# Splitting five mixer results in place, and sharing the first norm's scaling between two engines

## The chip, the core and the metric

The kernel runs on one core of one Trainium2 chip. The metric is the device time of one execution in microseconds. Lower is better.

## The reference

The reference computes two transformer-like blocks in float32 over a sequence of 1024 tokens with a width of 1024. The change lies in the first block. Sixteen learned tokens are put in front of the sequence, one input projection makes all the raw inputs, three mixers work side by side on parts of it, and their results are concatenated, projected and normalized:

```python
q_a, f_a, i_a, g_a, z_b, xbc_b, dt_b, u_c = jnp.split(h @ w_in[l], split_idx, axis=-1)
y_a = hgrn2_mixer(q_a, f_a, i_a, g_a, ...)      # 384 columns
y_b = mamba2_mixer(z_b, xbc_b, dt_b, ...)       # 384 columns, ends in an RMS norm per group
y_c = s5_mixer(u_c, ...)                        # 256 columns, ends in y * sigmoid(y @ glu_w + glu_b)
mixed = jnp.concatenate([y_a, y_b, y_c], axis=-1) @ w_out[l]
h = layer_norm(ALPHA * h + mixed, ln1_g[l], ln1_b[l])
ff = jnp.square(jax.nn.relu(h @ w_mlp_in[l])) @ w_mlp_out[l]
h = layer_norm(ALPHA * h + ff, ln2_g[l], ln2_b[l])
```

The second block (a gated delta rule, a spatial gating branch and a gated feed-forward part) follows with the same kinds of operations. It is not touched.

## The kernel before

The tokens are worked in two halves, h = 0 (with the 16 learned tokens, 528 columns) and h = 1 (512 columns). Results of mixers lie with channels on the 128 partitions and tokens along the free dimension. The concatenated 1024 channels of one half are eight tiles of 128x512: tiles 0 to 2 from HGRN2, 3 to 5 from Mamba2, 6 and 7 from S5's gate (`glu`).

The large products are done in three passes over two-part numbers. A float32 operand is split into `hi`, a rounded copy made by ScalarE (`act`), and `lo`, the difference, made by VectorE (`tt`). `split` (L216) does this for activations, in a tile of the pool `xt` with 16 buffers; `weights` (L223) does it for each weight tile after its load (raw `wr` with 2 buffers, `wh` and `wl` with 3 each); `mm3` (L233) issues the three matrix products for one pair. In the profile, `ps<-wh,xt` and `ps<-wl,xt` are such products of the output projection, where the activations are the stationary operand; `ps<-xt,wh` and `ps<-xt,wl` are those of the input projections and the first MLP matrix. `px` tiles are banks for the small products of mixers, transposes and sums.

Before the change every mixer writes its result tile to a buffer in device memory, `Y1[h][j]`, with a DMA issued on POOL's queue (L686 for Mamba2, L950 for the gate, L512 for HGRN2). `load_y` (L1185) reads all eight back on SP's queue into `ev` tiles, of which there are 5, and splits each:

```python
for j in range(8):
    raw = self.ev()[:, :512]
    self.nc.sync.dma_start(raw, Y[j])
    xs.append(self.split(raw, 512, f))
```

`out_proj` (L1199) multiplies the eight operands by the output matrix in two column halves of four weight pairs; pair kp uses operands 2kp and 2kp + 1 for four groups of 128 tokens, 24 products for each pair. `ln_first` (L1272) is the first norm of half 0: row statistics on VectorE and POOL, a normalizing pass on ScalarE, transposes on TensorE, and then for each of eight channel tiles a scale and shift straight from the transposed bank: once on ScalarE into `x.hi` (rounded), once on VectorE into `r` (exact), and a VectorE subtraction into `x.lo`.

`run` (L1477) writes the program as coroutines that are interleaved by hand. The first input projection (`p1`) runs beside S5 and the mixers of half 0 (`seq(0)`), then come the gate of half 0 (`glu(0)`), `new_acc` and `load_y`, then the output projection beside the mixers of half 1 (`mix1(1)`), the first norm, and the MLP beside the rest of `mix1(1)`. This order gives priorities only. When the kernel is built, the framework orders the instructions of each engine by priority and by when their operands and buffers come free, so what the trace shows on a queue can stand in another order than the code. Each engine then runs its queue in that order.

Of the kernel before, what the change touches and what calls it, by code (L numbers as in the profile page):

```python
# [14 lines left out]
AF = mybir.ActivationFunctionType  # L15
ALU = mybir.AluOpType
# [61 lines left out]
class Op:  # L78


    def __init__(self, hi, lo):
        self.hi, self.lo = hi, lo
# [5 lines left out]
class Kb:  # L88
    NF = 24

    def __init__(self, tc, es, ap):
        self.tc, self.nc, self.ap = tc, tc.nc, ap
        self.es = es
        self.n = 0
        ec = es.enter_context
        self.cst = ec(tc.tile_pool(name="cst", bufs=1))
        self.xtp = ec(tc.tile_pool(name="xtp", bufs=16))
        self.wp = ec(tc.tile_pool(name="wp", bufs=4))
        self.accp = ec(tc.tile_pool(name="accp", bufs=8))
        self.mx = ec(tc.tile_pool(name="mx", bufs=1))  # L100
        self.sm = ec(tc.tile_pool(name="sm", bufs=2))
        self.ps = ec(tc.tile_pool(name="ps", bufs=4, space=PSUM))
        self.px = ec(tc.tile_pool(name="px", bufs=4, space=PSUM))
        self.dr = ec(tc.tile_pool(name="dr", bufs=1, space=DRAM))
        nc = self.nc
        self.Y1 = [self.dram([8, 128, 512], "Y1") for _ in range(2)]
        self.Y2 = [self.dram([8, 128, 512], "Y2") for _ in range(2)]
        k = self.cst.tile([128, 8], F32, tag="k", name="k")
        for i, v in enumerate((RMS_EPS, math.log(128.0 ** -0.5), 1.0, math.pi / 2, -0.5)):
            nc.vector.memset(k[:, i:i + 1], v)  # L110
        self.eps_rms, self.lnq, self.one, self.hpi, self.mhalf = (k[:, i:i + 1] for i in range(5))
# [455 lines left out]
    def mamba(self, h):  # L567
        nc = self.nc
        NT, R0 = HW[h], T0[h]
        xs = [self.t(528) for j in range(3)]  # L570
# [19 lines left out]
        b = self.bank()  # L590
# [4 lines left out]
        Y = [self.t(512) for j in range(3)]  # L595
        for c in range(c0, 5):
# [14 lines left out]
            if c > 0:  # L611
                for hd in range(6):
                    self.ts(W[hd // 3][:, hd % 3, :], W[hd // 3][:, hd % 3, :], ac[:, 6 * c + hd:6 * c + hd + 1], ALU.subtract, 0.0, ALU.min)
                b = self.bank()
# [10 lines left out]
            b = self.bank()  # L625
# [8 lines left out]
            b = self.bank()  # L634
# [6 lines left out]
            if c > 0:  # L641
                yb = self.bank()
                for hd in range(6):
                    j, o = hd // 2, 64 * (hd % 2)
# [29 lines left out]
        for j in range(3):  # L674
            b = self.bank()
            if j == 0:
                self.sums(b, [(ones, sq[0], al), (ones[lo], sq[1], lo)])
            elif j == 1:
                self.sums(b, [(left, sq[0], al), (self.blk, sq[1], al), (right, sq[2], al)])
            else:  # L680
                self.sums(b, [(ones[up], sq[1], up), (ones, sq[2], al)])
            r = self.t(512)
            self.act(r, b, AF.Ln, scale=1.0 / 192, bias=self.eps_rms)
            self.act(r, r, AF.Exp, scale=-0.5)
            self.stt(Y[j], Y[j], self.col(P_NW1 + j), r, ALU.mult, ALU.mult)
            nc.gpsimd.dma_start(self.Y1[h][3 + j], Y[j])  # L686
            yield


# [241 lines left out]
    def glu(self, h):  # L931
        nc = self.nc
        j0 = 2 if h == 0 else 66
        gw = self.t(512)
        nc.sync.dma_start(gw.rearrange("p (k c) -> p k c", k=2), self.ap["gluw"])
        y = [self.t(524)[:, :512] for j in range(2)]
        for j in range(2):
            nc.sync.dma_start(y[j].rearrange("p (t j) -> p t j", t=8), self.yT[j][:, :, j0:j0 + 64])
            self.act(y[j], y[j], AF.Gelu_apprx_tanh)
        for m in range(2):  # L940
            b = self.bank()
            for k in range(2):
                self.mm(b, gw[:, 256 * k + 128 * m:256 * k + 128 * m + 128], y[k], k == 0, k == 1)
            s = self.t(520)[:, :512]
            self.act(s, b, AF.Tanh, scale=0.5, bias=self.s5gb[:, m:m + 1])
            o = self.t(528)[:, :512]
            p = lambda x: x.rearrange("p (t j) -> p j t", t=8)
            self.stt(o.rearrange("p (j t) -> p j t", t=8), p(s), 1.0, p(y[m]), ALU.add, ALU.mult)
            self.ts(o, o, 0.5, ALU.mult)
            nc.gpsimd.dma_start(self.Y1[h][6 + m], o)  # L950
            yield


# [228 lines left out]
            yield  # L1182


    def load_y(self, Y, f=False):  # L1185
        xs = []
        for j in range(8):
            raw = self.ev()[:, :512]
            self.nc.sync.dma_start(raw, Y[j])
            xs.append(self.split(raw, 512, f))  # L1190
        return xs
# [80 lines left out]
    def ln_first(self, acc, gb, xs):  # L1272

        nc = self.nc
        for a in acc:
            mean, rs = self.stats([a[:, 0:512], a[:, 512:1024]], "ln")
            nm = self.s("nm", 1, 4)
            self.stt(nm, mean, -1.0, rs, ALU.mult, ALU.mult)
            self.act(a, a, AF.Identity, scale=rs, bias=nm)
        for k in range(8):  # L1280
            b = self.bank()
            for t in range(4):
                nc.tensor.transpose(b[:, 128 * t:128 * t + 128], acc[t][:, 128 * k:128 * k + 128], self.ident)
            g, s = self.col(P_LN + k), self.col(P_LN + 8 + k)
            r, x = self.ev()[:, :512], self.xt()
            self.act(x.hi[:, :512], b, AF.Identity, scale=g, bias=s)
            self.ts(r, b, g, ALU.mult, s, ALU.add)
            self.tt(x.lo[:, :512], r, x.hi[:, :512].bitcast(F32), ALU.subtract)
            xs.append(x)
        yield  # L1290
        for hf in range(2):
            c = slice(512 * hf, 512 * hf + 512)
            rows = [self.ev()[:, :512] for _ in range(2)]
            for i in range(2):
                nc.sync.dma_start(rows[i], gb[i:i + 1, c].to_broadcast([128, 512]))
            for t in range(4):
                a = acc[t][:, c]
                self.tt(a, a, rows[0], ALU.mult)
                self.tt(a, a, rows[1], ALU.add)
                yield  # L1300
# [176 lines left out]
    def run(self):  # L1477
# [7 lines left out]
        p1, m = self.p1(), self.s5s()  # L1485
# [4 lines left out]
        m = self.both(m, self.seq(0))  # L1490
# [4 lines left out]
        st(self.glu(0))  # L1495

        a0 = self.new_acc(half(ap["x"], 0))
        ys = self.load_y(self.Y1[0])
        m = self.mix1(1)
        st(self.out_proj(ys, ap["wo1"], a0), 99, m, 0.75, False)  # L1500
        x0 = []
# [8 lines left out]
        ys = self.load_y(self.Y1[1], True)  # L1510
        st(q)
        a1 = self.new_acc(half(ap["x"], 1))
        o, x0, x1 = self.out_proj(ys, ap["wo1"], a1), [], []
# [3 lines left out]
        p, m, n = self.p2(0, x0), self.mix2(0), self.ln(a1, l1, xs=x1)  # L1517
# [7 lines left out]
        ys, hs, x1, x0 = self.load_y(self.Y2[0], True), [], [], []  # L1525
        st(q)
        n = self.ln(a1, l2, out=self.X2[1], xs=x1)
        g = self.merge(0, ys, hs)
        st(g, 99, n, 1, False)
        a0 = self.new_acc(self.X2[0])  # L1530
        o = self.out_proj(hs, ap["wo2"], a0)
        st(o, 4, n, 1)
        st(o, 99, n, 2)
        p, m, n = self.p2(1, x1), self.mix2(1), self.ln(a0, l3, xs=x0)
# [6 lines left out]
        ys, hs, x1 = self.load_y(self.Y2[1], True), [], []  # L1541
# [8 lines left out]
        n, r = self.ln(a0, l4, out=half(ap["out"], 0)), self.ffn(1, x1, a1, ((0, 4), (4, 4), (8, 4), (12, 4), (16, 2), (18, 4)),  # L1550
                                                              self.ln_last(a1, l4, half(ap["out"], 1)))
# [165 lines left out]
```

## Time and profile before

| what | value |
|---|---|
| median of 3 runs | 2798.53 us |
| lowest and highest run | 2794.23 and 2805.1 us |
| the profiled execution: its time | 2800.17 us |
| the profiled execution: its span, first to last instruction | 2798.3 us |
| mean granted TensorE clock | 0.99 |
| instructions | 37325 |

The time of an execution is a little above its span, because it also holds what lies before the first and after the last instruction. Engines are named PE (TensorE's products), PEld (its weight loads), DVE (VectorE), ACT (ScalarE), POOL (GpSimd) and SP (SyncE, which issues most DMAs; SPq is its queue).

### The profile page before, as it was taken

The numbers are of one execution on the slowest core, as the hardware profiler recorded it, in microseconds if no ns is written. First come the engines' busy times: TensorE is split into PE (matmuls) and PEld (weight loads), VectorE is DVE, ScalarE is ACT, GpSimd is POOL, SyncE is SP. The second block draws the span as 40 slices with busy tenths as digits, with TensorE's granted clock in tenths as the row PEclk, the third lists the DMA queues.
The fourth block names the chain that finished last, engine by engine and source line by source line (L and its number), as shares of the span: only waits on it lengthen the run. The fifth ranks groups of instructions, "written<-read, shape, count | busy, mean of one in ns | idle before, by whom it ended". The sixth has DMA issues, their size and how long they took to land.

```text
span 2798.3 us, 37325 instructions
## 1 busy us (share of the span) xinstructions
PE 2722.5 (97%) x14176; PEld 2261.6 (81%) x14176; DVE 1793.5 (64%) x3321; ACT 1162.4 (42%) x1810; POOL 220.4 (8%) x365
## 2 busy tenths in 40 slices
PE   7999988999999999999999999999999999999997
PEld 7788776778878888877888878888788888888886
DVE  7668768777756654376645665534867657675566
ACT  4334444444442353263323333534545434444442
POOL 3121001000001112010100001100100000000000
PEclk9999999999999999999999999999999999999999
DMA  7432463323344543333333455434234533343332
GB/s 213 130 98 84 138 186 106 117 87 102 111 146 153 164 151 122 121 116 118 120 95 122 141 161 182 142 125 136 83 108 148 170 98 110 109 143 98 98 95 79
DMA packets 138036, 351.55 MB, mean 126 GB/s; under 512 B 26779, under 2 KB 40641, under 8 KB 137857
## 3 DMA queue, kind: packets, MB, share of 16 engines
q1 hardware_dynamic: 113712, 295.34, 34.4%
q0 software_dynamic: 16672, 48.50, 5.1%
q10 hardware_dynamic: 7473, 5.34, 0.7%
q8 instruction: 111, 1.82, 0.3%
q14 instruction: 68, 0.56, 0.1%
HBM read 296.84 MB, written 51.69 MB: 125 GB/s over the span
## 4 chain that ended last, share of the span: by engine, by line
PE 76%; issue 8%; DVE 8%; DMA 4%; ACT 3%; POOL 1%; SPq 0%; DVEq 0%; POOLq 0%; ACTq 0%
PE ps L204 68%; PE px L204 7%; DVE f L192 2%; ACT f L189 2%; DVE wl L192 1%; DVE ta L192 1%; DVE f L195 1%; DMA ev<-gt 1%; PE px L1268 1%; DMA f<-rows 1%; DVE acc L195 1%; DMA wr<-in_w 1%; DMA cx<-qkv 1%; ACT wh L189 1%; DMA f<-in_xT 0%
## 5 line engine op out<-in xcount | busy, mean ns | idle before, releaser
L204 PE MATMUL ps<-xt,wh 128*128 128x512 f32 (+1 forms) x3616 | 1098.3, 382 | 8.9 <-ACT wh L189 8.7
L192 DVE TENSOR_TENSOR wl<-wr,wh 128x1024 fp32r<-128x1024 f32 (+3 forms) x431 | 521.9, 1211 | 581.7 <-ACT wh L189 566.3
L204 PE MATMUL ps<-wh,xt 128*128 128x512 f32 (+3 forms) x2624 | 804.3, 380 | 8.2 <-ACT xt L189 4.9
L189 ACT ACTIVATE wh<-wr 128x1024 fp32r<-128x1024 f32 (+3 forms) x431 | 452.2, 1050 | 863.6 <-PE ps L204 772.7
L204 PEld LDWEIGHTS ps<-xt,wh 128*128 128x128 f32 x3616 | 665.3, 189 | 123.4 <-ACT wh L189 8.6
L204 PE MATMUL ps<-xt,wl 128*128 128x512 f32 (+1 forms) x1808 | 683.9, 378 | 6.6 <-DVE wl L192 6.6
L204 PEld LDWEIGHTS ps<-wh,xt 128*128 128x128 f32 (+1 forms) x2624 | 486.0, 188 | 95.1 <-ACT xt L189 8.1
L204 PE MATMUL ps<-wl,xt 128*128 128x512 f32 (+3 forms) x1312 | 496.8, 379 | 1.1 <-DVE wl L192 1.0
L204 PEld LDWEIGHTS ps<-xt,wl 128*128 128x128 f32 x1808 | 341.8, 189 | 69.2 <-DVE wl L192 8.6
L204 PE MATMUL ps<-f,wh 128*128 128x512 f32 x960 | 293.5, 386 | 0.0
L204 PEld LDWEIGHTS ps<-wl,xt 128*128 128x128 f32 (+1 forms) x1312 | 247.3, 189 | 43.7 <-DVE wl L192 3.3
L189 ACT ACTIVATE f<-f 128x512 f32<-128x512 f32 (+6 forms) x300 | 178.8, 614 | 206.2 <-DVE f L192 62.6
L204 PE MATMUL px<-f,f 128*128 128x128 f32 (+8 forms) x1832 | 203.3, 259 | 20.4 <-DVE f L192 12.4
L204 PEld LDWEIGHTS ps<-f,wh 128*128 128x128 f32 x960 | 179.9, 187 | 36.3
L189 ACT ACTIVATE ev<-ps 128x512 f32<-128x512 f32 (+4 forms) x303 | 169.3, 561 | 64.7 <-PE ps L204 58.2
L192 DVE TENSOR_TENSOR acc<-acc,ps 128x512 f32<-128x512 f32 x192 | 131.0, 684 | 89.4 <-PE ps L204 88.4
L204 PE MATMUL ps<-f,wl 128*128 128x512 f32 x480 | 184.8, 385 | 0.0
L204 PEld LDWEIGHTS px<-f,f 128*128 128x128 f32 (+2 forms) x1192 | 133.7, 180 | 57.4 <-issue 25.3
L192 DVE TENSOR_TENSOR f<-f,f 128x256 f32<-128x256 f32 (+5 forms) x244 | 129.0, 549 | 38.4 <-ACT f L189 36.5
L189 ACT ACTIVATE xt<-ev 128x512 fp32r<-128x512 f32 x131 | 82.4, 629 | 152.4 <-DVE ev L192 147.3
L195 DVE SCALAR_TENSOR_TENSOR ev<-ev,p,ev 128x512 f32<-128x512 f32 x176 | 132.3, 752 | 2.7 <-ACT ev L189 0.6
L192 DVE TENSOR_TENSOR xt<-ev,xt 128x512 fp32r<-128x512 f32 x124 | 86.1, 697 | 50.7 <-ACT xt L189 50.3
(223 smaller groups left out, 2047.9 us busy)
## 6 DMA issues: line engine op xcount, KB each, us to landing
wr<-in_w SPq DMA_DIRECT2D x93, 512.0 KB, 3.8
wr<-in_wup SPq DMA_DIRECT2D x88, 512.0 KB, 3.5
wr<-in_wmi SPq DMA_DIRECT2D x64, 512.0 KB, 3.6
wr<-in_wmo SPq DMA_DIRECT2D x64, 512.0 KB, 3.7
wr<-in_wdn SPq DMA_DIRECT2D x44, 512.0 KB, 3.4
wr<-in_wo SPq DMA_DIRECT2D x32, 512.0 KB, 3.8
Y<-f POOLq DMA_DIRECT2D x32, 256.0 KB, 2.6
ev<-Y SPq DMA_DIRECT2D x32, 256.0 KB, 3.7
```

The lines of the kernel that those rows point to most:

```text
L189: self.nc.scalar.activation(out=out, in_=in_, func=func, **kw)
L192: self.nc.vector.tensor_tensor(out=out, in0=a, in1=b, op=op)
L195: self.nc.vector.scalar_tensor_tensor(out=out, in0=a, scalar=s, in1=b, op0=op0, op1=op1)
L204: self.nc.tensor.matmul(out, lhsT, rhs, start=start, stop=stop)
L1268: nc.tensor.transpose(b[:, 128 * t:128 * t + 128], acc[t][:, 128 * k:128 * k + 128], self.ident)
```

## The change

Two things are changed. For half 0 Mamba2's three results and the gate's two are split where they are made and kept as operands in `xt` tiles; they are not written to device memory, and `load_y` takes them from a table, so that it loads and splits only tiles 0 to 2. Half 1 is left as it was. In `ln_first`, for every second channel tile, the exact scaled copy `r` is made by ScalarE and not by VectorE.

```diff
+        self.ysp = {}
...
             self.stt(Y[j], Y[j], self.col(P_NW1 + j), r, ALU.mult, ALU.mult)
-            nc.gpsimd.dma_start(self.Y1[h][3 + j], Y[j])
+            if h == 0:
+                self.ysp[3 + j] = self.split(Y[j], 512)
+            else:
+                nc.gpsimd.dma_start(self.Y1[h][3 + j], Y[j])
...
             self.ts(o, o, 0.5, ALU.mult)
-            nc.gpsimd.dma_start(self.Y1[h][6 + m], o)
+            if h == 0:
+                self.ysp[6 + m] = self.split(o, 512)
+            else:
+                nc.gpsimd.dma_start(self.Y1[h][6 + m], o)
...
-    def load_y(self, Y, f=False):
+    def load_y(self, Y, f=False, made={}):
         xs = []
         for j in range(8):
+            if j in made:
+                xs.append(made[j])
+                continue
...
             self.act(x.hi[:, :512], b, AF.Identity, scale=g, bias=s)
-            self.ts(r, b, g, ALU.mult, s, ALU.add)
+            if k % 2:
+                self.act(r, b, AF.Identity, scale=g, bias=s)
+            else:
+                self.ts(r, b, g, ALU.mult, s, ALU.add)
...
-        ys = self.load_y(self.Y1[0])
+        ys = self.load_y(self.Y1[0], made=self.ysp)
```

## Rows read from the trace of the kernel before

**Rows 1.** The page: span; busy us of each engine, share of the span, xinstructions.

```profile
span 2798.3 us, 37325 instructions
...
PE 2722.5 (97%) x14176; PEld 2261.6 (81%) x14176; DVE 1793.5 (64%) x3321; ACT 1162.4 (42%) x1810; POOL 220.4 (8%) x365
```

**Rows 2.** Windows: us, busy PE, PEld, DVE, ACT, POOL (xinstructions), PE clock, DMA, GB/s.

```profile
0.00:490.00 490.00, 444.61 (x2729) 378.05 (x2730) 362.40 (x1022) 206.48 (x363) 75.33 (x139) 0.96 0.46 136
490.00:2730.00 2240.00, 2224.24 (x11214) 1839.60 (x11213) 1386.28 (x2229) 937.05 (x1422) 141.34 (x222) 1.00 0.40 125
```

**Rows 3.** Windows around the change, columns as in rows 2.

```profile
405.00:410.00 5.00, 2.43 (x8) 0.92 (x6) 2.54 (x3) 2.55 (x6) 1.07 (x2) 0.83 0.91 342
410.00:415.00 5.00, 4.42 (x10) 3.18 (x11) 2.15 (x4) 2.20 (x4) 0.00 (x0) 0.50 0.92 228
...
420.00:425.00 5.00, 3.98 (x15) 2.36 (x14) 2.19 (x4) 3.24 (x8) 0.54 (x1) 1.00 0.65 200
...
480.00:485.00 5.00, 4.21 (x16) 3.03 (x15) 2.95 (x6) 3.84 (x6) 0.00 (x0) 0.50 0.06 23
...
440.00:475.00 35.00, 33.06 (x184) 27.13 (x182) 34.70 (x77) 14.20 (x21) 1.12 (x2) 1.00 0.25 76
```

**Rows 4.** Waits of PE, 403 to 441 us: total, times, longest.

```profile
PE ps L204 <- ACT xt L189: 4.7, 3, 3.1
```

**Rows 5.** Timeline of PE: start, us, instruction, [idle before <-releaser].

```profile
404.95 0.34 PE L204 MATMUL ps<-wh,xt 128*128 128x390 f32 x1
...
410.58 0.79 PE L204 MATMUL ps<-wh,xt 128*128 128x512 f32 x1 [3.15 <-ACT xt L189]
...
423.15 3.70 PE L204 MATMUL px<-f,f 128*128 128x512 f32 x8 [1.02 <-ACT f L189]
...
435.66 0.48 PE L204 MATMUL ps<-wh,xt 128*128 128x512 f32 x1 [0.76 <-ACT xt L189]
...
438.12 0.50 PE L204 MATMUL ps<-wh,xt 128*128 128x512 f32 x1 [0.80 <-ACT xt L189]
```

**Rows 6.** The chain of waits, 425 to 441 us: start, us, what.

```profile
428.54 3.62 DMA Y<-f
...
432.17 2.79 DMA ev<-Y
...
434.98 0.64 ACT xt L189
```

**Rows 7.** Timelines of POOL's queue and of SP's queue, 380 to 440 us.

```profile
417.90 1.20 POOL L686 DMA_DIRECT2D Y<-f  x2 [11.05 <-DVE f L195]
...
430.25 0.54 POOL L950 DMA_DIRECT2D Y<-f  x1 [1.17 <-DVE f L199]
...
383.74 0.38 SPq L226 DMA_DIRECT2D wr<-in_wo  x1
...
420.25 4.03 SPq L1189 DMA_DIRECT2D ev<-Y  x3
...
424.80 0.42 SPq L362 DMA_DIRECT2D f<-sf  x1
```

**Rows 8.** Instruction groups, 404 to 495 us: busy, mean ns, idle before.

```profile
L192 DVE TENSOR_TENSOR xt<-ev,xt 128x512 fp32r<-128x512 f32 x16 | 10.7, 690 | 10.1 <-ACT xt L189 10.0
L201 DVE TENSOR_SCALAR ev<-px,p 128x512 f32<-128x512 f32 x8 | 6.1, 806 | 2.1 <-ACT xt L189 2.1
L189 ACT ACTIVATE xt<-px,p 128x512 fp32r<-128x512 f32 x8 | 5.8, 776 | 3.0 <-PE px L1283 2.9
...
L436 DVE COPY_PREDICATED f<-bm,px 128x256 f32<-128x256 uint8 x10 | 5.0, 569 | 0.1
L189 ACT ACTIVATE xt<-ev 128x512 fp32r<-128x512 f32 x8 | 5.0, 626 | 5.0 <-DMA ev<-Y 5.0
...
L192 DVE TENSOR_TENSOR f<-f,f 128x256 f32<-128x256 f32 x9 | 3.7, 420 | 0.0
```

**Rows 9.** Timeline of the first norm: PE's first product with its operands.

```profile
482.34 1.65 PE L204 MATMUL ps<-xt,wh 128*128 128x512 f32 x3 [0.23 <-ACT xt L189]
```

## The prediction

> **What bounds the kernel now.** I began with the page: TensorE is busy for 97% of the span, VectorE for 64% [rows 1]. Read alone, that says that only two things can move the time: TensorE's idle time, 2798.3 - 2722.5 = 75.8 us in all, and stretches in which its clock is granted at half. The next view is the same sum by stage [rows 2]. Up to 490 us TensorE is idle for 490 - 444.6 = 45.4 us. Between 490 and 2730 us it is idle for 2240 - 2224.2 = 15.8 us at a clock of 1.00. The rest, 14.6 us, is the tail. Everything that the change touches lies between 404 and 494 us, in the first kind of stage, so there is something to win there; what follows is full, so what is won there isn't easily lost or multiplied.
>
> Then I cut that stretch into slices of 5 us [rows 3]. The reader is to see the holes. From 405 to 410 us TensorE is idle for 2.6 us, and the slice after it is at 0.50, the lower of the clock's two levels (1.2 GHz of 2.4). From 420 to 425 it is idle for 1.0 us at full clock; a hole like it follows behind 434 us. The last is at the first norm, which ends in the slice from 480 to 485 at 0.50. The waits name who ended most of them up to 441 us [rows 4]: 4.7 us for ScalarE's halves of the operands (xt). The timeline gives each wait its place [rows 5]: 3.15 us before the first product of the output projection, 1.02 us for an activation before the gate's own products, 0.76 and 0.80 us before the products that use the operands 6 and 7. The chain of waits explains the last two [rows 6]: a store of a result of the gate (3.62 us), its load (2.79 us), and then the split.
>
> **The change part by part.** *Up to 417 us nothing moves.* Operands 0, 1 and 2 (HGRN2) are still stored, loaded and split as before, and the first instruction that is new stands where Mamba2's first store stood, at 417.90 us [rows 7]. So the wait of 3.15 us, which belongs to operand 0, stays, and so does the half clock after it. Cost and gain are 0; it could only go if the order of the queues became another before that point, which I keep as a rival.
>
> *Five results no longer go through memory.* Removed are five stores on POOL's queue and five loads on SP's. What is seen of them on TensorE: the gate's first result is ready when its store is issued, at 428.5 us [rows 6]. Split on the spot it is an operand after 0.626 us on ScalarE and 0.690 us on VectorE [rows 8], at about 429.9 us, and the second one, stored at 430.25 [rows 7], at 431.6. TensorE asks for them at 435.66 - 0.76 = 434.9 and 438.12 - 0.80 = 437.3 us [rows 5]. So both waits go, 0.76 + 0.80 = 1.56 us, with 5 us to spare. That is the lower bound of this part.
>
> The wait of 1.02 us is less sure. TensorE stands before the gate's products, which need the Gelu activations. Behind them in its queue lie the products with operand 3, whose load SP could begin only at 420.25 us, after the store [rows 7]. In the new kernel operand 3 can be had at 417.90 + 0.626 + 0.690 = 419.2 us, so its products (12 of the 24 of a weight pair) can fill the hole. Whether they are put ahead of the gate's products is decided by the framework, which orders each queue when the kernel is built; it can also leave the gate's products in front, and then nothing is won here. The part is worth 0 to 1.02 us. I take 1.02, since the order seen in the trace takes whatever is ready: SP issues weights of this projection at 383.74 us, though in the code the loads of its operands stand ahead of them [rows 7].
>
> *Who pays for the splits.* There are as many splits as before, five ScalarE copies and five VectorE subtractions (5 x 0.626 and 5 x 0.690 us), only earlier. From 415 to 425 us ScalarE has Mamba2's norm and the gate, and three copies more, 1.9 us, come among them. Behind them wait the weights of the last pair, which TensorE first touches at 435.66 us, and the Gelu activations. If these came 1.9 us later, the gate's second result would be there at 433.5, still ahead of 437.3. Cost 0 as long as that room lasts. The operand buffers can be had: 16 exist, and those of the first half of x were last read before the second value projection, which itself ends at 405 us [rows 5].
>
> *SP's queue.* The three loads of 420.25 hold SP for 4.03 us, and behind them wait the loads of the second half's HGRN2, issued from 424.80 [rows 7]. Without them those loads can go out at 420.25 us or before, so the second half's work starts 4.5 us earlier or more. VectorE has room for it, with 2.2 of 5 us busy from 420 to 425; from 440 to 475 it is full, with 34.7 of 35 us [rows 3]. This work is not on TensorE's path at that time, so I count it as 0, and it is the source of two rivals.
>
> *The first norm.* Before, each of the eight operand tiles takes ScalarE 0.776 us, and VectorE 0.806 + 0.690 us [rows 8]. VectorE sets the pace, with 8 x 1.496 = 12.0 us less overlap. After, four scalings change engine: VectorE has 4 x 0.806 = 3.2 us less, ScalarE 4 x 0.776 = 3.1 us more, about 9 us for each. But TensorE does not stand still for VectorE here. It waits 0.23 us before the first product [rows 9]; in the slice from 480 to 485 it is busy for 4.2 of 5 us [rows 3], since several weight tiles are open at once (the row shows three products in a run). So the gain is 0. The bounds: 0.23 us and half of a slice at half clock (4.2 / 2 = 2.1 us) at best; 3.1 us lost if ScalarE now held up the next tile.
>
> The Trainium skill (ScalarE: Activation LUTs, Rules for kernel authors) says that add and multiply belong on VectorE, not on ScalarE, which speaks against this edit. The rows here don't bear it out for this tile, 0.776 against 0.806 us [rows 8]; by the rule the sum would lose up to those 3.1 us.
>
> **The sum.** 1.56 + 1.02 = 2.6 us, of the profiled execution's 2800.2: 2797.6 us. That execution lies 1.6 us above the median of the runs, so the predicted median is 2796.0 us. From no change a measurement of this kernel tells about 0.5%, 14 us; the gain is a fifth of that.
>
> **The rivals.** *Given back.* VectorE is full from 440 to 475 us. If the norm's statistics come no sooner although the projection ends sooner, TensorE waits 2.6 us longer at the norm: 2798.5 us. For it speaks VectorE's 34.7 of 35 us; against it that the second half's work also moves ahead by several us.
>
> *Slower: the second half crowds the norm.* Its scores come in levels. One takes VectorE 5 operations on 256 columns and two masked copies, 5 x 0.420 + 2 x 0.569 = 3.2 us [rows 8]. If with the earlier loads one more level stands in VectorE's queue ahead of the norm's statistics, the gain is gone; from there on each costs its 3.2 us, with TensorE idle. Two give -2.6 + 6.4 = +3.8 us: 2802.3. It decides from the point at which the first product with the norm's tiles comes later than at 482.34 us, where it stands now [rows 9].
>
> *ScalarE holds the norm.* With the skill's rule taken at its word, 3.1 us lost, 2.6 gained: 2799.0 us. Against it: ScalarE is at work for less than VectorE on these tiles before.
>
> *More is won.* If the order changes before 417 us as well, the 3.15 us, half of the 4.4 us at 0.50 from 410 to 415 (2.2 us) and the norm's 2.1 us come on top: 2.6 + 7.4 = 10.0 us, 2788.5 us.
>
> *The order after 490 us is made anew.* A gain above 14 us needs 11.4 us out of the 15.8 + 14.6 us that TensorE idles there, a loss above 14 us nearly as many waits again as 490 to 2730 us has now. For it speaks only that every queue is ordered again.
>
> **How the numbers follow.** The forecast has 0.55; given back 0.11; crowded norm 0.11; ScalarE 0.02; more won 0.07; order anew 0.08 on the fast side and 0.06 on the slow side. The cases within 14 us make 0.86, faster 0.08, slower 0.06. The likeliest's own range is 2794 to 2798. The range for all reaches from the 2788.5 of "more is won" to the 2802.3 of the crowded norm, each widened by the 4 us by which the fastest run of before lies below the median: 2785 to 2806, and leaves out the order made anew and edges, under 0.2.
>
> **What would show it.** Right: in the profile after, no wait for operands 6 and 7 around 430 to 440 us; five stores and five loads of Y fewer; the wait of 3.15 us still there; the second half's first loads before 421 us; TensorE's idle time up to 490 us lower by 2 to 3 us. Wrong: a new wait above 3 us between 417 and 490 us, a longer stretch at 0.50 around the norm, or idle time from 490 to 2730 us that isn't near 16 us.

## The result

The change made the kernel slower. The changed kernel takes 2819.62 us (median of 6 runs, 2810.48 to 2824.66) against 2796.38 us for the kernel before beside it; the ratio is 1.007, with a 95% interval of 1.0056 to 1.0085 (the two medians alone give 1.0083). Forecast were 2796.0 us, 2785 to 2806, and a chance of 0.06 for slower by more than 14 us.

The profiled execution took 2817.59 us, 17.4 us more than the one of before. Its page, span and engines' busy time:

```profile
span 2815.7 us, 37288 instructions
...
PE 2727.1 (97%) x14176; PEld 2264.2 (80%) x14176; DVE 1792.5 (64%) x3317; ACT 1166.0 (41%) x1814; POOL 215.6 (8%) x360
```

TensorE's share of 97% is that of [rows 1]; the page doesn't show the loss. The windows do, with the columns of [rows 2]:

```profile
0.00:490.00 490.00, 436.06 (x2689) 370.26 (x2690) 354.56 (x1010) 200.10 (x354) 71.88 (x134) 0.95 0.45 131
...
410.00:415.00 5.00, 2.38 (x4) 1.12 (x4) 0.69 (x1) 3.69 (x7) 0.83 (x2) 0.50 0.93 244
415.00:420.00 5.00, 0.00 (x0) 0.00 (x0) 4.33 (x9) 3.06 (x8) 0.00 (x0) 0.50 1.01 264
420.00:425.00 5.00, 3.56 (x5) 1.60 (x6) 0.17 (x1) 1.15 (x2) 0.00 (x0) 0.52 0.00 1
...
430.00:435.00 5.00, 3.92 (x10) 2.82 (x11) 2.50 (x4) 3.14 (x6) 0.00 (x0) 0.66 0.00 0
```

Up to 490 us TensorE is busy for 436.1 us, 8.5 us less than in [rows 2]. The holes of [rows 3] were 1 to 2.6 us wide; now one slice is quite empty, the slices before and behind it run at 0.50 and 0.52, and after one at 1.00 the slice from 430 to 435 us is at 0.66. TensorE's waits from 380 to 500 us:

```profile
PE px L205 <- ACT f L190: 12.1, 2, 8.1
PE ps L205 <- ACT xt L190: 4.4, 2, 4.2
PE px L1293 <- ACT acc L190: 3.5, 3, 2.2
PE px L205 <- DVE f L193: 3.2, 2, 2.8
```

Its timeline gives them their places (all line numbers of the helpers are one higher than before; the last row is from a later stage, see below):

```profile
410.95 2.38 PE L205 MATMUL px<-f,o 128*128 128x512 f32 x4 [4.00 <-ACT f L190]
...
421.44 5.35 PE L205 MATMUL px<-f,f 128*128 128x512 f32 x8 [8.11 <-ACT f L190]
...
431.00 0.49 PE L205 MATMUL ps<-wh,xt 128*128 128x512 f32 x1 [4.21 <-ACT xt L190]
...
492.76 1.65 PE L205 MATMUL ps<-xt,wh 128*128 128x512 f32 x3 [0.23 <-ACT xt L190]
...
1366.07 1.38 PE L205 MATMUL px<-f,f 128*128 128x128 f32 x8 [2.26 <-DVE f L196]
```

The output projection's first product starts at 431.00 us and no longer at 410.58 [rows 5]: the products of operands 0 to 2, which used to fill the time up to the gate's products, can't be had, and TensorE stands in front of the gate's products (421.44) with nothing else to do. The norm's first product comes at 492.76 us, 10.4 us later than in [rows 9]. Why the splits come so late, ScalarE's timeline shows (the row at 1360.57 is for later):

```profile
425.11 0.69 ACT L190 ACTIVATE f<-px,s5gb 128x512 f32<-128x512 f32 x1 [3.20 <-PE px L205]
...
427.58 0.63 ACT L190 ACTIVATE xt<-f 128x512 fp32r<-128x512 f32 x1
...
429.80 0.63 ACT L190 ACTIVATE xt<-f 128x512 fp32r<-128x512 f32 x1 [1.58 <-DVE f L200]
430.33 1.66 ACT L190 ACTIVATE xt<-ev 128x512 fp32r<-128x512 f32 x3
...
1360.57 0.59 ACT L190 ACTIVATE f<-px 128x512 f32<-128x512 f32 x1
```

The three `xt<-ev` are the splits of operands 0 to 2, the ones still loaded. They stand right behind the two splits of the gate (`xt<-f`). SP's queue says when their loads were issued, and the view of the loads' line how long each took until it had landed:

```profile
403.85 5.66 SPq L1199 DMA_DIRECT2D ev<-Y  x3
...
414.40 1.31 SPq L363 DMA_DIRECT2D f<-sf  x1
```

```profile
DMA to landing us min/median/max: 4.2/5.2/6.1
```

The loads were issued from 403.85 us on, the last at 409.2 us. With the longest of these times all data were there by 415.3 us at the latest, 15 us before the splits. Nothing of the data was late; the splits stood in a queue behind instructions that waited for the gate. The Trainium skill (TensorE: Matmul & The Clock Gate, the table at its head) calls ScalarE's queue strictly first in, first out; the trace agrees: ScalarE stood idle for 3.20 us before 425.11, with the three splits ready behind.

A second loss shows further on. From the first load of the `wsg` weights to the last of the `wmi` weights (917.3 to 1536.6 us before, 926.3 to 1551.2 after) the changed kernel takes 624.8 us against 619.4. The longest wait there that before has not is that of 2.26 us at 1366.07 above, in the spatial gating of the second block, which nobody touched. VectorE's row says whom it waited for, POOL's rows why:

```profile
1365.27 0.75 DVE L196 SCALAR_TENSOR_TENSOR f<-f,sgm,f 128x512 f32<-128x512 f32 x1 [2.47 <-POOL sgm L1161]
```

```profile
1357.48 0.79 POOL L1187 DMA_DIRECT2D Y<-f  x1 [3.27 <-ACT f L190]
1363.90 0.75 POOL L1187 DMA_DIRECT2D Y<-f  x1 [5.63 <-ACT wh L190]
1364.67 0.56 POOL L1161 TENSOR_TENSOR sgm<-sgm,k 128x1 f32<-128x1 f32 x1
```

The store at 1363.90 is the third of four. What it stores was ready when ScalarE's copy ended, 1360.57 + 0.59 = 1361.2 us, so it goes out 2.7 us late (the releaser named is a weight split, which the store doesn't read). The power for the row statistics (`sgm`) stands behind it on POOL, and VectorE and TensorE behind that. In the kernel before the same 2.8 us fall on the second store, ready at 1346.3 us, with no power behind it at once:

```profile
1349.17 0.79 POOL L1180 DMA_DIRECT2D Y<-f  x1 [5.74 <-issue]
1350.72 0.75 POOL L1180 DMA_DIRECT2D Y<-f  x1 [0.77 <-ACT f L189]
1351.49 0.97 POOL L1154 TENSOR_TENSOR sgm<-sgm,k 128x1 f32<-128x1 f32 x1
```

So of the 17.4 us, 9.1 are there at the first `wsg` load and 5.4 more at the last `wmi` load. The other 2.9 us come behind it, where TensorE is idle for as long as before (22.1 against 21.9 us) and has a lower clock in places, such as 0.98 against 1.00 from 1750 to 1850 us.

### The profile page after: what moved, and what is told of

Its sections match the earlier page's. It is cut to its first block, busy times and chain, and to the rows that moved or that the text cites. A ratio compares the mean times of both kernels' runs of the same rounds, so it can differ in the third digit from the quotient of the medians.

```text
span 2815.7 us, 37288 instructions
## 1 busy us (share of the span) xinstructions
PE 2727.1 (97%) x14176; PEld 2264.2 (80%) x14176; DVE 1792.5 (64%) x3317; ACT 1166.0 (41%) x1814; POOL 215.6 (8%) x360
## 4 chain that ended last, share of the span: by engine, by line
PE 81%; DVE 7%; issue 5%; DMA 5%; ACT 3%; POOL 1%; SPq 0%; DVEq 0%; POOLq 0%; ACTq 0%
PE ps L205 72%; PE px L205 8%; DVE f L193 2%; ACT f L190 2%; DMA f<-rows 2%; DVE wl L193 1%; DVE f L196 1%; DMA cx<-qkv 1%; PE px L1278 1%; DMA hx<-ev 1%; DMA wr<-in_w 1%; DVE acc L196 1%; ACT wh L190 0%; DMA vdt<-ev 0%; DVE f L437 0%
## 5 line engine op out<-in xcount | busy, mean ns | idle before, releaser
L193 DVE TENSOR_TENSOR f<-f,f 64x256 f32<-64x256 f32 (+5 forms) x244 | 129.5, 552 | 40.9 <-ACT f L190 38.1
```

The costliest lines, as they stand in the source:

```text
L193: self.nc.vector.tensor_tensor(out=out, in0=a, in1=b, op=op)
```

## The experiments

The question for the first four: is it the first edit or the second, and is it the work of the splits, their place in the code, or how their tiles are had? Each ratio is against the kernel before, run beside it on the same chip.

**1. The norm's edit alone** (the kernel before, with the second edit only).

> Only the second edit (ScalarE makes the exact copy of every second tile in the first norm), on the kernel before. Theory A, the loaded operands queue behind the gate's because operand tiles are handed out in the order of the code: this edit has no part in the loss, within 5 us of the kernel before, and the two waits of 8.1 and 4.2 us before the output projection don't appear. Theory B, the norm edit reorders ScalarE's queue and costs most of the 20 us: 10 us or more above the kernel before.

Measured: 2786.63 us, ratio 1.000 (0.999 to 1.001). The waits before the first product (3.80 us), the gate's products (1.01) and operands 6 and 7 (0.25 and 0.79) stand at the places of [rows 5]; those of 8.1 and 4.2 us don't appear. The norm's edit is neither the loss nor a gain.

**2. The splits in place alone** (the changed kernel without `if k % 2`).

> Only the first edit (five results split in place), the norm as before. Theory A: the whole loss, 15 to 25 us above the kernel before, with waits near 8 and 4 us on TensorE between 410 and 431 us. Theory B: less than 7 us above.

Measured: 2804.55 us, 1.0061 (1.0049 to 1.0073), with waits of 8.3 and 4.2 us at the same places. The loss is the first edit's.

**3. Another pool for the loaded operands.** The changed kernel; only the tiles of operands 0 to 2 come from the accumulators' pool, under the name `xy`. Their place in the code and all work stay.

```diff
+            if made:
+                x = self.accp.tile([128, 2, 528], F32R, tag="acc", name=self.nm("xy"))
+                x = Op(x[:, 0], x[:, 1])
...
             xs.append(self.split(raw, 512, f))
```

> The changed kernel, but the three operands that are still loaded get tiles of another pool (the accumulators', which has three free). Loads, splits and their place in the code stay. Theory A (order within one pool): the three splits come back to 409 to 418 us, ahead of the gate's; the waits of 8.1 and 4.2 us go; 15 to 23 us below the changed kernel, that is 0 to 5 us below the kernel before. Theory C (ScalarE takes what stands first in the code, and the three stand behind the gate there): the splits stay behind the gate's at 430 us and the time stays at that of the changed kernel, within 4 us.

Measured: 2786.93 us, 0.9994 (0.9983 to 1.0005). ScalarE's queue is another one:

```profile
399.82 0.62 ACT L190 ACTIVATE xy<-ev 128x512 fp32r<-128x512 f32 x1
...
406.09 1.15 ACT L190 ACTIVATE xy<-ev 128x512 fp32r<-128x512 f32 x2
407.38 0.64 ACT L190 ACTIVATE xt<-f 128x512 fp32r<-128x512 f32 x1
...
417.81 1.15 ACT L190 ACTIVATE xt<-f 128x512 fp32r<-128x512 f32 x2 [1.90 <-DVE f L200]
```

The loaded operands are split 10 us and more ahead of the gate's, and TensorE's waits for operands are down to one of 2.7 us before the first product. Same work, same place in the code, another pool: the loss is gone. So it was neither the splits' own work nor the place of the instructions in the code as such. Nor was the common pool short of buffers: in experiment 4 it holds the same eight operands.

**4. The loads and splits of operands 0 to 2 ahead of Mamba2's final norm in the code**, in the common pool.

```diff
+        if h == 0:
+            for j in range(3):
+                raw = self.ev()[:, :512]
+                nc.sync.dma_start(raw, self.Y1[0][j])
+                self.ysp[j] = self.split(raw, 512)
         sq = []
```

> The changed kernel, but the three loads and splits stand in the code ahead of Mamba2's norm, in the same pool as before. Theories A and C alike: the waits of 8.1 and 4.2 us go. The operands are there before the projection can begin, so the wait of 3.15 us of the kernel before goes too, with the half clock after it: 3 to 10 us below the kernel before. Theory D, the loss comes from the splits that ScalarE and VectorE now do in this stretch: still 10 us or more above the kernel before.

Measured: 2785.89 us, 0.9996 (0.9982 to 1.0009). TensorE's waits from 380 to 500 us:

```profile
PE px L1298 <- ACT acc L190: 5.7, 3, 4.0
PE px L205 <- DVE f L193: 0.7, 1, 0.7
PE ps L205 <- ACT xt L190: 0.2, 1, 0.2
```

Of the waits before the norm none above 0.7 us is left, and at the first `wsg` load this kernel is 6.5 us ahead of experiment 1, on the same chip. At the end it is ahead by 0.6 us, and its median is 1.6 us below that of the kernel before, less than the 3 to 10 us expected. The gain is there and is given back later; so is a lead of 3.8 us in experiment 3. Both have the wait of 2.3 us in the spatial gating, experiment 1 hasn't.

**5. The five stores kept.** The kernel of experiment 4, and the five results are also stored on POOL's queue as before. Nothing reads these copies. The edit for Mamba2's three (the gate's two likewise):

```diff
             if h == 0:
                 self.ysp[3 + j] = self.split(Y[j], 512)
-            else:
-                nc.gpsimd.dma_start(self.Y1[h][3 + j], Y[j])
+            nc.gpsimd.dma_start(self.Y1[h][3 + j], Y[j])
```

> The kernel with the loads and splits of operands 0 to 2 ahead of Mamba2's final norm, and besides that the five results are stored to DRAM on POOL's queue as before (nothing reads these copies). It is for the 5 to 6 us that every kernel with the first edit loses again between 905 and 1530 us: there POOL issues one store of the spatial gating about 2.8 us after its data are ready, in the kernel before and in the norm-only kernel the second of the four stores, in all kernels without the five stores the third, which stands ahead of the power of the row statistics for which TensorE then waits 2.3 us. Theory E: the late issue comes after a fixed amount of transfers on POOL's queue, so five fewer stores move it by one store. Then with the five stores back it falls on the second store again, TensorE's wait of 2.3 us at the last rows of the spatial gating goes, the clock stays at 1.0 behind it, the lead of about 6 us at 905 us is kept, and the time is 0.997 to 0.9985 of before. Theory F: the late issue or the loss comes from the order of the queues that the first edit makes anew; then the wait of 2.3 us stays and the time is 0.999 to 1.001 of before.

Measured: 2784.22 us, 0.9973 (0.9961 to 0.9985), the best so far. POOL's queue in the spatial gating, and the product that waited:

```profile
1333.26 0.79 POOL L1190 DMA_DIRECT2D Y<-f  x1 [5.78 <-issue]
1334.75 0.75 POOL L1190 DMA_DIRECT2D Y<-f  x1 [0.71 <-ACT f L190]
1335.52 0.98 POOL L1164 TENSOR_TENSOR sgm<-sgm,k 128x1 f32<-128x1 f32 x1
```

```profile
1337.34 1.16 PE L205 MATMUL px<-f,f 128*128 128x128 f32 x8 [0.33 <-DVE f L196]
```

The late store is the second again, ready at 1330.4 us and issued 2.8 us after, and the wait is 0.33 us. Five transfers some 900 us earlier decide which store is late. With work added that nobody needs, the ratio is lower than in experiment 4 by 0.0023; the two intervals just touch (0.9982 to 0.9985).

**6 and 7. Only the gate's two, or only Mamba2's three results split in place**; the others are stored and loaded.

> The changed kernel with only the gate's two results split in place; Mamba2's three are stored and loaded as before. Theory A (the splits of the loaded operands queue on ScalarE behind those written before them in the code, which wait for the gate): all six loaded operands now stand behind the gate's two splits, so the output projection's first product still starts about 20 us after 410 us and the waits of about 8 and 4 us are there; 1.004 to 1.008 of before. Rival (the loss grows with the number of results split in place): two of five give about 0.4 of the loss, 1.002 to 1.004. Of the late store in the spatial gating: where it is the third of the four, TensorE waits over 2 us there; where it is the second, it doesn't.

> The changed kernel with only Mamba2's three results split in place; the gate's two are stored and loaded as before. Theory A: operand 0's split stands behind Mamba2's third split, 418.8 us in the changed kernel, instead of 409.9, so the first product starts at about 420 us, the wait before it is 5 to 9 us, and the time is 1.001 to 1.005 of before, less than with the gate's two alone. Rival (loss by the number of results): three of five give 0.6 of the loss, 1.004 to 1.0055, more than with the gate's two alone. Of the late store: as for the gate's two alone.

Measured: the gate's two 2798.61 us, 1.0026 (1.0014 to 1.0039); Mamba2's three 2792.58 us, 1.0004 (0.9992 to 1.0017). First TensorE with the gate's two, then ScalarE with Mamba2's three:

```profile
414.16 5.65 PE L205 MATMUL px<-f,f 128*128 128x512 f32 x8 [5.06 <-ACT f L190]
...
424.01 0.49 PE L205 MATMUL ps<-wh,xt 128*128 128x512 f32 x1 [4.20 <-ACT xt L190]
```

```profile
413.93 0.63 ACT L190 ACTIVATE xt<-f 128x512 fp32r<-128x512 f32 x1 [0.28 <-DVE f L196]
414.46 0.61 ACT L190 ACTIVATE xt<-ev 128x512 fp32r<-128x512 f32 x1
```

Two results cost more than three (the ends of the intervals overlap), so the loss doesn't go by their number; it goes by the latest split that stands ahead. The time with the gate's two alone, 1.0026, would fit the rival; the order of the two times doesn't, and the waits stand where theory A puts them. With Mamba2's three operand 0 is split right behind Mamba2's last, as foretold, and the wait before the first product is 6.8 us, within the 5 to 9 foretold. But both times came out lower than expected. In both the late store is the second, without the wait there, which is 0.001 of it; the rest of the difference I can't name.

**8. The three tiles taken early, written late.** The changed kernel, with `self.xt()` for operands 0 to 2 called ahead of Mamba2's final norm; loads and splits stay in `load_y`.

> The changed kernel, with the three operand tiles of the loaded results taken from the pool ahead of Mamba2's final norm in the code, but loaded and written where they were. Theory A as first stated (the order goes by where the code takes a tile from the pool): the splits come ahead of the gate's and the waits of 8.1 and 4.2 us go, 0.998 to 1.001 of before. Theory A2 (the order goes by where the code first writes a tile of the pool): all waits stay, 1.0055 to 1.0085 of before, as the changed kernel.

Measured: 2806.03 us, 1.0053 (1.0039 to 1.0067). The waits stay:

```profile
PE px L205 <- ACT f L190: 11.9, 2, 8.0
PE ps L205 <- ACT xt L190: 4.4, 2, 4.2
```

So the theory as I first stated it is wrong in one word. Taking a tile from the pool decides nothing; where the code first writes it does. This rule is worked out from experiments 3, 4 and 8; how the framework comes to it, no run shows.

**9, 10 and 11. The five stores kept in other kernels**: in the changed kernel, in that of experiment 3, and in that of experiment 5 without the norm's edit.

> The changed kernel, with the five results also stored on POOL's queue as before (nothing reads these copies); the splits of the loaded operands still stand last. Theory: the changed kernel's loss has two parts, some 15 us from the order of the splits and some 5 us from the late store that stands ahead of the power of the row statistics. Then the waits of about 8 and 4 us stay, the late store is the second again, TensorE's wait of 2.3 us at the spatial gating goes, and the time is 1.003 to 1.006 of before. Rival: the order of the splits is the whole loss and the wait of 2.3 us is made up elsewhere; then 1.006 to 1.008.

> The kernel whose loaded operands take their tiles from the accumulators' pool, with the five results also stored on POOL's queue as before. Theory E (the late issue is moved by the number of transfers on POOL's queue): the late store is the second again, no wait of 2.3 us, and the time goes from 0.9994 to 0.996 to 0.9985 of before. Rival (the gain with the loads first came from their place in the code, not from the stores): 0.999 to 1.001.

> The kernel with the loads first and the five stores kept, without the edit of the norm. If the norm's edit is worth nothing, as alone (1.000), the time stays at 0.996 to 0.9985 of before. Rival (with the operands earlier the norm's copies on VectorE set the pace, and the edit takes effect): 0.999 to 1.001, and the norm's first product starts later than 467 us.

Measured: 1.0032 (1.0019 to 1.0045) with 2795.95 us; 0.9989 (0.9977 to 1.0001) with 2784.98 us; 0.9978 (0.9967 to 0.999) with 2782.39 us. In the changed kernel with the stores the waits of the first loss are still there:

```profile
PE px L205 <- ACT f L190: 11.3, 2, 7.5
PE ps L205 <- ACT xt L190: 4.4, 2, 4.2
```

In all three the late store is the second, and the wait of 2.3 us is gone. The norm's edit is worth nothing here either (0.9978 without, 0.9973 with it). The other pool with the stores gained only 0.0005, less than forecast: 0.9989 lies between the theory's range and the rival's, and the time alone decides nothing here. The trace has the stretch of the table below shorter by 2.3 us, 619.0 against 621.3.

All kernels together, by which of the four stores is late, with the time from the first `wsg` to the last `wmi` load:

| kernels | late store | us |
|---|---|---|
| after, 2, 3, 4, 8 | third | 624.8, 624.2, 621.3, 623.2, 622.6 |
| before, 1, 5, 6, 7, 9, 10, 11 | second | 619.4, 618.7, 619.2, 620.4, 619.2, 621.9, 619.0, 619.1 |

The means are 623.2 and 619.6: the third costs 3.6 us, 2.3 of them the wait. The rest goes with the clock behind the wait. In the changed kernel it is 0.84 from 1360 to 1370 us, and in 2 and 4 it falls as far; in 3 and 8 it stays at 1.00, and their mean, 622.0, is above 619.6 by about the wait. The two rows of the table overlap (3 and 9), so a single kernel proves little here. By the times, keeping the stores is worth 0.0038, 0.0023 and 0.0005 in the three pairs, 0.0022 or 6 us on average; the two kernels of a pair were not run side by side, and the difference of two such ratios is known to about 0.002.

## Why the prediction failed

**"Up to 417 us nothing moves"** is the step that failed. I looked for what is new in time, and found the first new instruction at 417.90 us. But the operands 0 to 2, whose instructions are the same as before, share a pool with five tiles that the code now writes ahead of them. Before, all eight were written in `load_y`, in the order in which their data come. In the changed kernel the pool's order puts the gate's two, ready last, in front of the loaded three, ready first. The other pool (experiment 3) and the earlier writing (4) each undo it; mere taking (8) doesn't. So the first product, which was to stay at 410.58 us, came at 431.00, behind waits of 8.1 and 4.2 us. That the framework takes whatever is ready, as I wrote from SP's rows, is true only within that order.

**"The operand buffers can be had: 16 exist"** asked the wrong question of the same fact: whether there is room, and not in which order it is given.

**The two waits for operands 6 and 7** (1.56 us) went, as said: in the changed kernel no wait for operands of this projection is left beside the first (the other 0.2 us of that row are the norm's). **The wait of 1.02 us** before the gate's products became 8.1, because the products meant to fill it were held up too; with the order mended (3 and 4) it is gone. **The wait of 3.15 us** was to stay; it is 2.7 in experiment 3, behind another of 2.6 at Mamba2's norm, and with the earlier code (4) it goes as well. So the mechanism of the forecast was right for what it looked at, with the order mended: the lead is 3.8 us in experiment 3, where 2.6 were forecast, and 6.5 in 4, on the way to the 10.0 of "more is won".

**"Only earlier, cost 0"** for the splits holds for their work (3 has the same work at 0.9994). **SP's queue:** the second half's loads came at 414.40 in place of 424.80 us, as said. **The norm's edit at 0:** right, alone (1.000) and in the best kernel. By the rule of the Trainium skill (ScalarE: Activation LUTs, Rules for kernel authors) up to 3.1 us were to be lost, 0.001; experiment 1, at 0.999 to 1.001, can't exclude that but gives it no support.

**The rivals.** The slower one, a crowded norm, did not happen. Its sign, a first product later than 482.34 us, did come (492.76), but from the waits ahead of it: the wait at the norm is 0.23 us, as before. "Given back" happened in 3 and 4, but not where I put it: at a store 900 us later, moved there by stores that are no longer issued. "The order made anew" had the right place, past 490 us, and the wrong cause: the late store follows what was stored before it and not the order of queues. The sign named for a wrong forecast, a new wait above 3 us between 417 and 490 us, is what came, twice.

What stays open is what POOL does in the 2.8 us. What decides on which store they fall, the traces narrow down. All these stores are of 256 KB, so if transfers or bytes were counted, five stores fewer would move the late one by five; it moved by one. A store of the spatial gating writes 4 x 128 pieces of 512 bytes, one of the five 128 rows of 2 KB. Counted in such pieces, five stores are 640, 1.25 of the others, three (7) are 0.75 and two (6) 0.5, which fits a move by one, none and none. I added up the pieces of all transfers on POOL's queue, as the trace lists them with each: in all thirteen kernels the late store is the one with which the sum passes a number between 28816 and 28944. Counted in POOL's instructions, no one number fits. No run was made to test the count; four stores fewer, 512 pieces, weren't tried. The Trainium skill (DMA: Bandwidth & Descriptors, SWDGE vs HWDGE vs iDMA) says that GpSimd writes the descriptors of such transfers into rings in SBUF; no run here shows a ring.

## What to carry to other kernels

When some of several tiles of one pool are made earlier or by another producer, ask in which order the code now writes the pool's tiles: one that is ready late and written first holds up those that are ready early, on an engine that has nothing to do with it. Write them in the order in which they become ready, or give the late ones a pool of their own, and read the engine's queue after the change, instruction by instruction, ahead of any sum. When a lead of a few microseconds at one place is gone at the end, compare the leads at fixed landmarks, such as the first load of a certain weight: here that found a late store 900 us further on, which five stores more or fewer move to a harmless place.

## What the runs showed of the hardware

A store on POOL's queue is issued 2.7 to 2.8 us after its data are ready, once in the second block of every kernel here, on a store that moves with the pieces stored ahead of it: all thirteen kernels fit one sum of pieces, near 28900. On one store it costs TensorE hardly a wait, on the next, by the means, 3.6 us. The first block has one more such issue, in all thirteen kernels on the same store, which takes the sum from 15120 to 15248. In the changed kernel its data were ready at 261.05 + 0.37 = 261.4 us and it went out 2.0 us later:

```profile
261.05 0.37 ACT L190 ACTIVATE ev<-ps 128x264 f32<-128x264 f32 x1
```

```profile
263.46 0.55 POOL L293 DMA_DIRECT2D sxbc<-ev  x1 [7.16 <-issue]
```

The granted clock at one and the same place differs from execution to execution. From 2000 to 2050 us, the kernel of experiment 7, that of experiment 9 and the kernel before, in windows:

```profile
2000.00:2050.00 50.00, 48.12 (x362) 37.97 (x361) 36.24 (x69) 17.52 (x31) 0.00 (x0) 1.00 0.27 85
```

```profile
2000.00:2050.00 50.00, 48.11 (x355) 37.66 (x354) 37.91 (x74) 17.66 (x30) 0.00 (x0) 0.97 0.23 75
```

```profile
2000.00:2050.00 50.00, 48.13 (x349) 37.62 (x348) 36.55 (x71) 16.96 (x29) 0.00 (x0) 0.93 0.24 74
```

No edit touches this place. TensorE is idle for 1.9 us in each, and the clock is 1.00, 0.97 and 0.93. Much of the scatter of one kernel's executions goes with the clock: of 29 runs of the kernel before, beside experiment 1, the five with a mean clock of 0.990 took 2794.1 us on average and the four with 0.994 took 2785.7. So a difference of a few microseconds between two profiled executions is read at landmarks ahead of such a place, or from many runs.
